# Two edits to a two-layer backbone kernel: the modulation's gates are stored as rows, once per layer, and the output projection multiplies 512 columns per product

## The chip, the cores and the metric

The kernel runs on one core of one Trainium2 chip. The metric is the device time of one execution in microseconds (us). The kernel before takes 1515.74 us, the median of three runs (1512.39, 1515.74 and 1519.95). The profile is that of one further execution, which took 1514.81 us.

The core has a matrix engine (PE in the profile, with its weight loads as PEld), a vector engine (DVE), a scalar engine (ACT), a general engine (POOL), and a synchronising engine (SP) that here only issues transfers. Each runs its own list of instructions in order and waits on semaphores for the others.

## What is computed

Two layers of a backbone over 512 latent tokens and 256 context tokens, 1024 channels wide. Cut to what the change touches:

```python
def trunk_layer(x, xc, mod, mod_c, ...):
    shift, scale, gate = jnp.split(mod[:, None, :], 3, axis=-1)
    shift_c, scale_c, gate_c = jnp.split(mod_c[None, None, :], 3, axis=-1)
    z = split_columns((rmsnorm(x, pre_g) * (1 + scale) + shift) @ w_in)
    ...
    out = merge_branches(z, y_mla, y_pool, y_gla, w_branch_mla, w_branch_pool, w_branch_gla, w_out)
    x = x + gate * rmsnorm(out, post_g)
    if with_ctx_out:
        ...
        xc = xc + gate_c * rmsnorm(out_c, post_g)
    return x, xc

def merge_branches(zz, y_mla, y_pool, y_gla, w_bm, w_bp, w_bg, w_out):
    ...
    merged = g_mla * (y_mla @ w_bm) + g_pool * (y_pool @ w_bp) + g_gla * (y_gla @ w_bg)
    return merged @ w_out

def reference(...):
    for l in range(DEPTH):
        mod = silu_c @ mod_w[l] + mod_b[l]
        mod_c = silu_cc @ mod_w[l] + mod_b[l]
        x, xc = trunk_layer(x, xc, mod, mod_c, ..., l < DEPTH - 1)
```

The gates are `gate` and `gate_c`, the last third of the modulation: 1024 numbers for the latent stream and, in layer 0 only, 1024 for the context stream. The output projection is `merged @ w_out`, 1024 by 1024, over 768 tokens in layer 0 and 512 in layer 1.

## The kernel before

**Products.** Every large product is taken in three: both factors are split into a high and a low part, and `mm3` adds high by high, high by low and low by high into the same PSUM tile (L89 is the one line that issues them). A weight block comes by an SP transfer into a `raw` tile (3 buffers), ACT rounds it to the high part (names that begin with `wh`, L68), and DVE subtracts for the low part (`wl`, L71). There are 4 buffers each for `wh` and `wl`. A product with 128 tokens as the stationary side writes a tile of 128 tokens by as many columns as the weight block is wide.

**Order.** The program is written stage by stage, but a scheduler with a model of times lays out each engine's list, so that work of a later stage (the loads above all) is put between that of an earlier one, and a change of one stage can move instructions of others.

**Modulation.** `mod` is computed in twelve chunks of 256 columns per layer, in the order 0, 4, 1, 5, 2, 6, 3, 7, 8, 9, 10, 11. In layer 0 the first eight run on PE at the start of the program; chunks 8 to 11 of layer 0 (the gates) and all of layer 1 run beside PE: POOL and DVE multiply the weights (`raw_mod`) by one number per partition (L231) and sum them in `macc`, and two small products `modt` turn the sum into columns. `columns(j)` adds the bias and, for the gates, multiplies by the post norm; its result goes to the tile `mcols`, channel `b*128 + p` at partition `p`, column `b`. For the chunks 8 to 11 it then stores the two new columns of each stream to `grow`, an array of rows of 1024 in the chip's memory (L180). Four chunks by two streams make 8 such stores in layer 0, four chunks of one stream make 4 in layer 1.

**Gate rows.** At the start of the output projection `gate_rows` reads `grow` back by POOL, each row broadcast over all 128 partitions (`pg<-grow`, L265): twice in layer 0, once in layer 1.

**Output projection.** `mh` and `ml` are the two parts of the merged activations, with the channels `k` (8 blocks of 128) on the partitions. The weights lie in four column blocks of 256. The first half takes the two blocks of columns 0 to 511 one after the other; in each, the tokens go in pairs of tiles, (2,3), (4,5) and in layer 0 also (0,1), and each pair runs `k` 0 to 5 for both tiles before `k` 6 and 7. ACT copies each tile's 256 columns to `part`. The second half (`wo2` tiles, `wo` in the profile) takes tile after tile, 2 times 256 columns in one PSUM tile. Behind each tile of the second half the norm, the gate (`pg`) and the residual (`xres`, L1069) are applied. In layer 0, `emit_hT` then turns each pair of tiles into columns for layer 1: per `k` two transposes on PE (`xT`, L1098), a scale and shift on DVE (`hv`, L1101), and its high part on ACT (`hh`) and low part on POOL (`hl`).

Of the kernel before, what the change touches and what calls it, by code (L numbers as in the profile page):

```python
# [11 lines left out]
F32 = mybir.dt.float32  # L12
# [6 lines left out]
P = 128  # L19
D = 1024  # L20
KD = 8
# [4 lines left out]
DEPTH = 2  # L26
# [22 lines left out]
def hybrid_kernel(ctx, tc, io, out):  # L49
    nc = tc.nc  # L50
    V, S, G, PE = nc.vector, nc.scalar, nc.gpsimd, nc.tensor
# [8 lines left out]
    stage = ctx.enter_context(tc.tile_pool(name="stage", bufs=2))  # L60
    small = ctx.enter_context(tc.tile_pool(name="small", bufs=4))
    dram = ctx.enter_context(tc.tile_pool(name="dram", bufs=1, space=MemoryType.DRAM))
    psz = ctx.enter_context(tc.tile_pool(name="psz", bufs=2, space=MemoryType.PSUM))
# [3 lines left out]
    def act(out, in_, func=AF.Copy, **kw):  # L67
        return S.activation(out=out, in_=in_, func=func, **kw)  # L68
# [22 lines left out]
    def mm3(out, lh, ll, rh, rl, start, stop):  # L91
        mm(out, lh, rh, start, False)
        mm(out, lh, rl, False, False)
        mm(out, ll, rh, False, stop)
# [17 lines left out]
    def load_split(src, nk, width, name, pool=stream):  # L112
# [4 lines left out]
            split(h, l, raw)  # L117
        return h, l

    def load_block(src, width, name):  # L120

        return [load_split(src[:, 4 * i:4 * i + 4, :], 4, width, f"{name}_{i}") for i in range(2)]
# [32 lines left out]
    def modulation(l, pool=None):  # L155


        cols = const.tile([P, 24, 2], F32, tag=f"mcols{l}", name=f"mcols{l}")
        grow = dram.tile([2, D], F32, name=f"grow{l}")
        mods[l] = (cols, grow)  # L160
        modb = small.tile([P, 24], F32, tag="modb", name=f"modb{l}", bufs=1)
        nc.gpsimd.dma_start(out=modb, in_=io["mod_b"][l])
# [5 lines left out]
        def columns(j, pt, streams=2):  # L168

            at = slice(2 * j, 2 * j + 2)  # L170
            dst = cols[:, at, 0:streams]

            def spread(v, c0):
                return v[:, 2 * j - c0:2 * j - c0 + 2].unsqueeze(2).to_broadcast([P, 2, streams])

            tt(dst, pt[:, :, 0:streams], spread(modb, 0), ALU.add)
            if j >= 8:
                tt(dst, dst, spread(post, 16))
                for st in range(streams):
                    nc.gpsimd.dma_start(out=grow[st].rearrange("(b p) -> p b", p=P)[:, 2 * j - 16:2 * j - 14], in_=dst[:, :, st])  # L180
            elif j >= 4:

                stt(dst, dst, 1.0, spread(pre, 8), ALU.add, ALU.mult)
# [58 lines left out]
        for j in (0, 4, 1, 5, 2, 6, 3, 7, 8, 9, 10, 11):  # L242
            if pool is not None and j < 8:
                chunk_on_pe(j)
            else:
                pend.append(chunk_beside_pe(j))
                next(pend[-1])
                if len(pend) > 1:
                    next(pend.pop(0), None)
            if j == 11 or (pool is None and j == 7):  # L250
                yield
                for chunk in pend:
                    next(chunk, None)
                pend = []
            yield

    mods = {}

    def gate_rows(l, pool, streams):

        grow = mods[l][1]
        res = []
        for s in range(streams):
            pgt = pool.tile([P, D], F32, tag=f"pg{s}", name=f"pg{l}_{s}", bufs=1)
            nc.gpsimd.dma_start(out=pgt, in_=grow[s].partition_broadcast(P))  # L265
            res.append(pgt)
        return res

# [81 lines left out]
    def layer(l, hT, close_hT, side, todo_mod):  # L350
# [683 lines left out]
        part = op.tile([P, NT, 512], F32, tag="part", name=f"part{l}", bufs=1)  # L1034
        order = [2, 3, 4, 5] + ([0, 1] if full else [])
        mT = (mh, ml)
        for b in range(2):
            blk = load_block(io["w_out"][l, b], 256, f"wo{l}_{b}")
            for pair in zip(order[0::2], order[1::2]):
                pss_ = [(psz if t % 2 else psw).tile([P, 256], F32, tag="z" if t % 2 else "w", name=f"zB_wo{l}_{b}_{t}")  # L1040
                        for t in pair]

                for ks in (range(6), range(6, KD)):
                    for t, ps in zip(pair, pss_):
                        for k in ks:
                            wh, wl = blk[k // 4]
                            ts = slice(t * P, t * P + P)
                            mm3(ps, mh[:, k, ts], ml[:, k, ts], wh[:, k % 4, :], wl[:, k % 4, :], k == 0, k == KD - 1)
                for t, ps in zip(pair, pss_):
                    act(part[:, t, b * 256:b * 256 + 256], ps)  # L1050
        ssqs = small.tile([P, NT, 2], F32, tag="ssq_out", name=f"ssq_out{l}", bufs=1)

        for t in order:
            junk = op.tile([P, D], F32, tag="xo", name=f"junk{l}_{t}")
            act(junk[:, 0:512], part[:, t, :], AF.Square, scale=D ** -0.5, accum_out=ssqs[:, t, 0:1])
            tt(part[:, t, :], part[:, t, :], pgr[1 if t < 2 else 0][:, 0:512])
        blks = [load_block(io["w_out"][l, b], 256, f"wo{l}_{b}") for b in (2, 3)]
        xhs = {}
        for t in order:
            ps = psw.tile([P, 512], F32, tag="w", name=f"wo2_{l}_{t}")  # L1060
            ts = slice(t * P, t * P + P)
            for b in range(2):
                for k in range(KD):
                    wh, wl = blks[b][k // 4]
                    mm3(ps[:, b * 256:b * 256 + 256], mh[:, k, ts], ml[:, k, ts], wh[:, k % 4, :], wl[:, k % 4, :],
                        k == 0, k == KD - 1)
            xt = op.tile([P, D], F32, tag="xres", name=f"xres{l}_{t}", bufs=4)
            src = io["ctx"][t * P:t * P + P] if t < 2 else (io["x"] if l == 0 else x1_d)[(t - 2) * P:(t - 1) * P]
            nc.gpsimd.dma_start(out=xt, in_=src)  # L1069
            xo = op.tile([P, D], F32, tag="xo", name=f"xo{l}_{t}")  # L1070
            act(xo[:, 512:], ps, AF.Square, scale=D ** -0.5, accum_out=ssqs[:, t, 1:2])
            tt(xo[:, 512:], ps, pgr[1 if t < 2 else 0][:, 512:])
            ms = small.tile([P, 1], F32, tag="ms1", name=f"ms_post{l}_{t}")

            stt(ms, ssqs[:, t, 0:1], 16 * EPS, ssqs[:, t, 1:2], ALU.add, ALU.add)
            r = small.tile([P, 1], F32, tag="r1", name=f"r_post{l}_{t}")
            tt(r, ms, mhalf[:, 0:1], ALU.pow, G)
            stt(xo[:, 0:512], part[:, t, :], r, xt[:, 0:512], ALU.mult, ALU.add)
            stt(xo[:, 512:], xo[:, 512:], r, xt[:, 512:], ALU.mult, ALU.add)
            if not full:  # L1080
                nc.sync.dma_start(out=out[(t - 2) * P:(t - 1) * P], in_=xo)
                continue
            if t >= 2:
                nc.sync.dma_start(out=x1_d[(t - 2) * P:(t - 1) * P], in_=xo)
            xhs[t] = xhat_tile(xo, xt, op, f"x{l + 1}_{t}")
            if t % 2 == 1:
                emit_hT(nhT, mods[l + 1][0], xhs, t - 1, 2, op)
# [98 lines left out]
def _layout(inp):  # L1186
# [3 lines left out]
    def kblocks(w, n):  # L1190

        dp, kk, nn = w.shape
        return w.reshape(dp, kk // P, P, nn // n, n).transpose(0, 3, 2, 1, 4)
# [36 lines left out]
    d["gla_norm"] = cols(a["gla_norm"])  # L1230
    for n, s in (("m", "mla"), ("p", "pool"), ("g", "gla")):
        d[f"w_branch_{n}"] = kblocks(a[f"w_branch_{s}"], 256)
    d["w_out"] = kblocks(a["w_out"], 256)
    return {f"in_{k}": np.ascontiguousarray(v) for k, v in d.items()}


# [19 lines left out]
```

## Time and profile before

| | us |
|---|---|
| median of three runs | 1515.74 |
| the profiled execution | 1514.81 |
| its span, first to last instruction | 1513.0 |
| around the span | 1.8 |
| PE busy (8940 matmuls) | 1444.7 |
| DVE busy | 1066.7 |
| ACT busy | 717.3 |
| POOL busy | 521.8 |
| mean granted TensorE clock | 0.984 of full |

Matmuls overlap one another in the pipeline, so the spacing of their starts, not their own length, is what one costs. "<-" with a name after a comma gives what ended an idle time; in the view of windows each engine's busy time in the stretch is followed by its count of instructions, then by the granted clock, the share of the 16 DMA engines' time that was taken, and the rate in GB/s. A transfer's landing time is counted from its issue.

### The profile page before, as it was taken

The numbers are of one execution on the slowest core, as the hardware profiler recorded it, in microseconds if no ns is written. First come the engines' busy times: TensorE is split into PE (matmuls) and PEld (weight loads), VectorE is DVE, ScalarE is ACT, GpSimd is POOL, SyncE is SP. The second block draws the span as 40 slices with busy tenths as digits, with TensorE's granted clock in tenths as the row PEclk, the third lists the DMA queues.
The fourth block names the chain that finished last, engine by engine and source line by source line (L and its number), as shares of the span: only waits on it lengthen the run. The fifth ranks groups of instructions, "written<-read, shape, count | busy, mean of one in ns | idle before, by whom it ended". The sixth has DMA issues, their size and how long they took to land.

```text
span 1513.0 us, 23911 instructions
## 1 busy us (share of the span) xinstructions
PE 1444.7 (95%) x8940; PEld 1279.7 (85%) x8940; DVE 1066.7 (71%) x1980; ACT 717.3 (47%) x1340; POOL 521.8 (34%) x695
## 2 busy tenths in 40 slices
PE   7999999999997999997999999999999999998988
PEld 4799899998886889886879988988988888886778
DVE  3645999757576788876676373789976676686783
ACT  6554453343334445666443345654253555454532
POOL 3432333444243443542111064414463100053550
PEclk9999999999998999998999999999999999999999
DMA  9333323256544532346565234334356523157731
GB/s 366 108 125 113 107 96 115 90 166 192 183 74 101 144 118 90 130 147 163 173 210 198 82 126 129 124 127 127 100 180 204 164 96 96 51 151 145 232 132 69
DMA packets 64195, 209.75 MB, mean 139 GB/s; under 512 B 12464, under 2 KB 15696, under 8 KB 64080
## 3 DMA queue, kind: packets, MB, share of 16 engines
q1 hardware_dynamic: 38688, 116.74, 25.2%
q0 software_dynamic: 24528, 88.34, 18.3%
q10 hardware_dynamic: 864, 3.15, 0.5%
q8 instruction: 70, 1.15, 0.3%
q14 instruction: 45, 0.37, 0.1%
HBM read 161.65 MB, written 46.54 MB: 138 GB/s over the span
## 4 chain that ended last, share of the span: by engine, by line
PE 63%; issue 11%; DVE 11%; DMA 8%; POOL 3%; ACT 3%; POOLq 0%; DVEq 0%; SPq 0%; ACTq 0%
PE zA_m L89 13%; PE zB_gv L89 5%; PE zA_px L89 4%; PE zA_mg L89 4%; PE zB_wo L89 4%; PE wo L89 3%; DMA raw_m<-in_w_in 3%; PE lv L89 3%; PE zA_pg L89 3%; PE zA_gk L89 2%; PE br_p L89 2%; PE br_m L89 2%; PE br_g L89 2%; PE zB_qkv L89 2%; PE zA_gq L89 2%
## 5 line engine op out<-in xcount | busy, mean ns | idle before, releaser
L89 PE MATMUL zA_m<-hh,wh_m 128*128 128x512 f32 (+1 forms) x576 | 206.6, 359 | 1.0 <-ACT wh_m L68 1.0
L89 PE MATMUL zA_m<-hh,wl_m 128*128 128x512 f32 (+1 forms) x576 | 206.7, 359 | 0.6 <-DVE wl_m L71 0.6
L89 PE MATMUL zA_m<-hl,wh_m 128*128 128x512 f32 (+1 forms) x576 | 206.5, 359 | 0.0
L89 PEld LDWEIGHTS zA_m<-hh,wh_m 128*128 128x128 f32 x576 | 110.1, 191 | 16.0 <-ACT wh_m L68 1.4
L89 PEld LDWEIGHTS zA_m<-hh,wl_m 128*128 128x128 f32 x576 | 109.9, 191 | 15.6 <-DVE wl_m L71 1.1
L89 PEld LDWEIGHTS zA_m<-hl,wh_m 128*128 128x128 f32 x576 | 109.9, 191 | 14.4
L68 ACT ACTIVATE wh_m<-raw_m 128x1024 fp32r<-128x1024 f32 x48 | 50.9, 1060 | 93.0 <-PE zA_m L89 45.5
L68 ACT ACTIVATE pe<-sc,mx 128x768 f32<-128x768 f32 (+1 forms) x80 | 65.2, 814 | 60.2 <-DVE mx L831 59.7
L831 DVE TENSOR_REDUCE mx<-sc 128x1 f32<-128x768 f32 (+1 forms) x80 | 67.7, 846 | 34.7 <-PE sc L89 34.0
L71 DVE TENSOR_TENSOR wl_m<-raw_m,wh_m 128x1024 fp32r<-128x1024 f32 x48 | 59.0, 1228 | 45.6 <-ACT wh_m L68 45.1
L231 POOL TENSOR_SCALAR raw_mod<-raw_mod,csil 128x256 f32<-128x256 f32 x64 | 69.2, 1085 | 62.0 <-DVE macc L74 38.5
L74 DVE SCALAR_TENSOR_TENSOR macc<-raw_mod,csil,macc 128x256 f32<-128x256 f32 x132 | 70.8, 547 | 12.4 <-POOL macc L71 10.5
L68 ACT ACTIVATE pth<-pt 128x256 fp32r<-128x256 f32 (+1 forms) x144 | 61.8, 471 | 34.6 <-PE pt L853 34.0
L71 DVE TENSOR_TENSOR ptl<-pt,pth 128x256 fp32r<-128x256 f32 (+1 forms) x144 | 72.6, 534 | 7.2 <-ACT pth L68 6.2
L89 PEld LDWEIGHTS lv<-pqk 128*128 128x128 f32 x560 | 70.8, 191 | 4.7 <-issue 1.8
L347 POOL DMA_DIRECT2D sm<-st_m x32 | 17.6, 550 | 165.5 <-ACT st_m L68 148.1
L89 PE MATMUL lv<-pqk 128*128 128x128 f32 x560 | 73.4, 275 | 1.3 <-DVE pqk L71 1.2
L89 PE MATMUL sc<-kth,qth 96*128 96x256 f32 (+1 forms) x144 | 50.8, 353 | 19.0 <-ACT pe L68 18.9
L71 POOL TENSOR_TENSOR macc<-macc,raw_mod 128x256 f32<-128x256 f32 x64 | 55.1, 860 | 36.4 <-DVE macc L74 30.6
L89 PE MATMUL br_p<-yp,wh_wbp 128*128 128x512 f32 (+1 forms) x192 | 56.3, 376 | 8.6 <-ACT yp L68 6.8
L853 PE MATMUL pt<-ident,pe 128*128 128x128 f32 x416 | 61.3, 273 | 0.7 <-ACT pe L68 0.7
L89 PE MATMUL zB_gv<-wh_gv,hh 128*128 128x256 f32 x192 | 55.7, 291 | 4.1 <-ACT st_gv L68 2.1
(402 smaller groups left out, 4732.8 us busy)
## 6 DMA issues: line engine op xcount, KB each, us to landing
raw_mod<-in_mod_w SPq DMA_DIRECT2D x48, 512.0 KB, 5.0
raw_m<-in_w_in SPq DMA_DIRECT2D x48, 512.0 KB, 3.8
sm<-st_m POOLq DMA_DIRECT2D x24, 384.0 KB, 2.9
raw_wo<-in_w_out SPq DMA_DIRECT2D x16, 512.0 KB, 4.0
sm<-st_m POOLq DMA_DIRECT2D x24, 256.0 KB, 2.5
raw_gv<-in_w_gv SPq DMA_DIRECT2D x8, 512.0 KB, 4.6
raw_gg<-in_w_in SPq DMA_DIRECT2D x8, 512.0 KB, 4.0
raw_px<-in_w_in SPq DMA_DIRECT2D x8, 512.0 KB, 3.7
```

The source lines that it names most:

```text
L68: return S.activation(out=out, in_=in_, func=func, **kw)
L71: return (eng or V).tensor_tensor(out=out, in0=a, in1=b, op=op)
L74: return V.scalar_tensor_tensor(out=out, in0=a, scalar=s, in1=b, op0=op0, op1=op1)
L89: PE.matmul(out=out, lhsT=lhsT, rhs=rhs, start=start, stop=stop)
L231: G.tensor_scalar(out=w, in0=w, scalar1=c, scalar2=None, op0=ALU.mult)
L347: nc.gpsimd.dma_start(out=dst[:, lo:T], in_=st[:, lo:T])
L831: V.tensor_reduce(out=mx, in_=ps[:, 0:nkey], axis=AX.X, op=ALU.max, negate=True)
L853: PE.transpose(out=pt[:, kk, :], in_=pe[:, (k0 + kk) * P:(k0 + kk + 1) * P], identity=ident)
```

## The change

First, `columns` no longer stores anything. Once per layer, when chunk 11 has been finished, PE transposes the gate columns in `mcols` (16 of them in layer 0, 8 in layer 1) into a PSUM tile `gateT` of 16 (8) rows of 128 numbers (L262), ACT copies it to the tile `gates`, and one POOL transfer stores those rows to `grow` (L265), whose layout becomes block, stream, channel within the block. The reading back is now one transfer per stream with rows of 128 numbers, 512 bytes, where it was one row of 4 KB; in layer 1, with one stream, the eight pieces lie one behind the other as before.

Second, the output projection's weights are laid out by the host as two halves of 512 columns, each in four quarters of the rows (two `k` each), so that a transfer still brings 512 KB and there are still 8 in each layer. A pair of token tiles goes through the quarters together: both tiles take the two `k` of a quarter before the next quarter, with products 512 columns wide. `part` is written by one ACT copy per tile instead of two. The second half uses the kernel's existing `z_B` with the same blocks.

```diff
+    def load_wide(src, name):
+
+        return [load_split(src[i], 2, 512, f"{name}_{i}") for i in range(4)]
...
-        grow = dram.tile([2, D], F32, name=f"grow{l}")
+        grow = dram.tile([KD, 2 if l < DEPTH - 1 else 1, P], F32, name=f"grow{l}")
...
             if j >= 8:
                 tt(dst, dst, spread(post, 16))
-                for st in range(streams):
-                    nc.gpsimd.dma_start(out=grow[st].rearrange("(b p) -> p b", p=P)[:, 2 * j - 16:2 * j - 14], in_=dst[:, :, st])
...
+            if j == 11:
+
+                n = KD * grow.shape[1]
+                pt = psz.tile([n, P], F32, tag="z", name=f"gateT{l}")
+                columns_ = cols[:, 16:24, :].rearrange("p b s -> p (b s)") if n > KD else cols[:, 16:24, 0]
+                PE.transpose(out=pt, in_=columns_, identity=ident)
+                row = stage.tile([P, P], F32, tag="st", name=f"gates{l}")
+                act(row[0:n], pt)
+                nc.gpsimd.dma_start(out=grow.rearrange("b s p -> (b s) p"), in_=row[0:n])
...
-            nc.gpsimd.dma_start(out=pgt, in_=grow[s].partition_broadcast(P))
+            nc.gpsimd.dma_start(out=pgt.rearrange("q (b p) -> q b p", p=P), in_=grow[:, s].partition_broadcast(P))
...
-        for b in range(2):
-            blk = load_block(io["w_out"][l, b], 256, f"wo{l}_{b}")
-            for pair in zip(order[0::2], order[1::2]):
-                pss_ = [(psz if t % 2 else psw).tile([P, 256], F32, tag="z" if t % 2 else "w", name=f"zB_wo{l}_{b}_{t}")
-                        for t in pair]
-
-                for ks in (range(6), range(6, KD)):
-                    for t, ps in zip(pair, pss_):
-                        for k in ks:
-                            wh, wl = blk[k // 4]
-                            ts = slice(t * P, t * P + P)
-                            mm3(ps, mh[:, k, ts], ml[:, k, ts], wh[:, k % 4, :], wl[:, k % 4, :], k == 0, k == KD - 1)
-                for t, ps in zip(pair, pss_):
-                    act(part[:, t, b * 256:b * 256 + 256], ps)
+        blk = load_wide(io["w_out"][l, 0], f"wo{l}_0")
+        for pair in zip(order[0::2], order[1::2]):
+            pair = [(t, (psz if t % 2 else psw).tile([P, 512], F32, tag="z" if t % 2 else "w", name=f"zB_wo{l}_0_{t}"))
+                    for t in pair]
+
+            for i, (wh, wl) in enumerate(blk):
+                for t, ps in pair:
+                    for k in (2 * i, 2 * i + 1):
+                        ts = slice(t * P, t * P + P)
+                        mm3(ps, mh[:, k, ts], ml[:, k, ts], wh[:, k % 2, :], wl[:, k % 2, :], k == 0, k == KD - 1)
+            for t, ps in pair:
+                act(part[:, t, :], ps)
...
-        blks = [load_block(io["w_out"][l, b], 256, f"wo{l}_{b}") for b in (2, 3)]
+        blk = load_wide(io["w_out"][l, 1], f"wo{l}_1")
...
-            for b in range(2):
-                for k in range(KD):
-                    wh, wl = blks[b][k // 4]
-                    mm3(ps[:, b * 256:b * 256 + 256], mh[:, k, ts], ml[:, k, ts], wh[:, k % 4, :], wl[:, k % 4, :],
-                        k == 0, k == KD - 1)
+            ps = z_B(blk, 0, 512, mT, t, f"wo{l}_1", psw, "w")
```

The scheduler lays the engines' lists out anew. Three places show how.

POOL, in layer 0's attention, where the gate chunks are computed beside PE (`sm` stores a merge gate, `raw_mod` and `macc` are the modulation's weights and sums). Before, at chunk 9, with the stores of chunk 8:

```order
L347 DMA sm_550<-st_m_0_6328 128x768
L231 TENSOR_SCALAR raw_mod_9_0_6333<-raw_mod_9_0_6333,csil 128x256
L180 DMA grow_126<-mcols_125 128x2x1 x2
L71 TENSOR_TENSOR macc_9_6332<-macc_9_6332,raw_mod_9_0_6333 128x256
L231 TENSOR_SCALAR raw_mod_9_0_6333<-raw_mod_9_0_6333,csil 128x256
```

And now, behind chunk 11, where layer 1's chunk 0 has begun (its L233 is L231 of before):

```order
L343 DMA sm_551<-st_m_0_6664 128x768
L890 DMA sgm_0_4466<-sgm_546 128x768
L166 DMA modb_6742<-in_mod_b 128x24
L170 DMA post_6746<-in_post_norm 128x8
L233 TENSOR_SCALAR raw_mod_0_0_6749<-raw_mod_0_0_6749,csil 128x256
L265 DMA grow_126<-gates_6677 16x128
```

Eight stores of 128 by 2 single numbers, spread over four chunks, are now one store of 16 rows behind the last of them.

DVE, in layer 1, where the output projection begins (`mgt_late` and `acc` merge the branches, `ml` is the low part of a merged block `k`). Before, ahead of the first two `ml`:

```order
L71 TENSOR_TENSOR acc_4_14595<-acc_4_14595,mgt_late_15029 128x512
L71 TENSOR_TENSOR wl_wo_1_1_15378<-raw_wo_1_1_15375,wh_wo_1_1_15377 128x1024
L71 TENSOR_TENSOR ml_15164<-acc_1_14592,mh_15163 128x512
L71 TENSOR_TENSOR acc_6_14597<-acc_6_14597,mgt_late_15031 128x512
L71 TENSOR_TENSOR acc_7_14598<-acc_7_14598,mgt_late_15031 128x512
L71 TENSOR_TENSOR ml_15164<-acc_3_14594,mh_15163 128x512
```

And now:

```order
L74 SCALAR_TENSOR_TENSOR mgt_late_14729<-mgt_late_14729,br_m_256_14923 128x512
L71 TENSOR_TENSOR ml_14862<-acc_1_14288,mh_14861 128x512
L71 TENSOR_TENSOR acc_4_14291<-acc_4_14291,mgt_late_14727 128x512
L74 SCALAR_TENSOR_TENSOR mgt_late_14729<-mgt_late_14729,br_m_256_14931 128x512
L71 TENSOR_TENSOR wl_wo_0_3_14972<-raw_wo_0_3_14969,wh_wo_0_3_14971 128x1024
L71 TENSOR_TENSOR ml_14862<-acc_3_14290,mh_14861 128x512
```

The first `ml` stood behind three `acc` sums of the even blocks and the low part of a weight block; now it stands ahead of that weight block and of the sum of block 4.

PE, in layer 0, at the end of the output projection, where the products of the last token tile end (`xT` are the transposes for layer 1, `zA_gq` is layer 1's first product). Before:

```order
L89 MATMUL wo_0_1_9534<-wh_wo_3_1_9079,ml_8014 128x256
L1098 MATMUL xT_2_9425<-ident,xres_4_9324 128x128
L1098 MATMUL xT_2_9425<-ident,xres_5_9392 128x128
L1098 MATMUL xT_3_9432<-ident,xres_4_9324 128x128
L1098 MATMUL xT_3_9432<-ident,xres_5_9392 128x128
```

And now:

```order
L89 MATMUL zB_wo_1_1_9254<-wh_wo_1_3_8919,ml_8010 128x512
L1101 MATMUL xT_4_9039<-ident,xres_2_8948 128x128
L1101 MATMUL xT_4_9039<-ident,xres_3_8992 128x128
L1101 MATMUL xT_5_9046<-ident,xres_2_8948 128x128
L1101 MATMUL xT_5_9046<-ident,xres_3_8992 128x128
L1101 MATMUL xT_6_9053<-ident,xres_2_8948 128x128
L1101 MATMUL xT_6_9053<-ident,xres_3_8992 128x128
```

Before, the last product has the transposes of tiles 4 and 5 from `k` = 2 behind it; those of tiles 2 and 3 and two of tiles 4 and 5 stand among the products. Now four groups of the tiles 2 and 3 (`k` 4 to 7) and all of the tiles 4 and 5 stand behind the last product, seven groups (the first three of the tiles 4 and 5 among them) ahead of layer 1's first one.

More of the change, by code (lines that the diff above doesn't have):

```diff
@@ L1056, in layer @@
             tt(part[:, t, :], part[:, t, :], pgr[1 if t < 2 else 0][:, 0:512])
-        blks = [load_block(io["w_out"][l, b], 256, f"wo{l}_{b}") for b in (2, 3)]
+        blk = load_wide(io["w_out"][l, 1], f"wo{l}_1")
         xhs = {}
         for t in order:
-            ps = psw.tile([P, 512], F32, tag="w", name=f"wo2_{l}_{t}")
-            ts = slice(t * P, t * P + P)
-            for b in range(2):
-                for k in range(KD):
-                    wh, wl = blks[b][k // 4]
-                    mm3(ps[:, b * 256:b * 256 + 256], mh[:, k, ts], ml[:, k, ts], wh[:, k % 4, :], wl[:, k % 4, :],
-                        k == 0, k == KD - 1)
+            ps = z_B(blk, 0, 512, mT, t, f"wo{l}_1", psw, "w")
             xt = op.tile([P, D], F32, tag="xres", name=f"xres{l}_{t}", bufs=4)
@@ L1232, in _layout @@
         d[f"w_branch_{n}"] = kblocks(a[f"w_branch_{s}"], 256)
-    d["w_out"] = kblocks(a["w_out"], 256)
+    d["w_out"] = a["w_out"].reshape(DEPTH, 4, 2, P, 2, 512).transpose(0, 4, 1, 3, 2, 5)
     return {f"in_{k}": np.ascontiguousarray(v) for k, v in d.items()}
```

## Prediction

> **What bounds the kernel now.** First the page's head, its busy times and its chain of work that ended last:
>
> ```profile
> span 1513.0 us, 23911 instructions
> PE 1444.7 (95%) x8940; PEld 1279.7 (85%) x8940; DVE 1066.7 (71%) x1980; ACT 717.3 (47%) x1340; POOL 521.8 (34%) x695
> PE 63%; issue 11%; DVE 11%; DMA 8%; POOL 3%; ACT 3%; POOLq 0%; DVEq 0%; SPq 0%; ACTq 0%
> ```
>
> PE is the bound, at 95%: only 1513.0 − 1444.7 = 68 us are left in which it does nothing, and DMA has 8% of the chain, a large share for an engine whose work should be ahead. So a change can win in two ways: fewer microseconds of products, or fewer of those 68. I therefore went to the waits of PE and asked of each long one what ended it and what stood before. The longest is at 452 us, in layer 0's attention. Here the waits of the stretch 440 to 465 (us in total, times, longest), POOL's row ahead of it in the timeline, and the transfer's landing time, in that stretch and as the median of the whole run:
>
> ```profile
> PE sc L89 <- ACT pe L68: 10.2, 1, 10.2
> ACT wh_m L68 <- DMA raw_m<-in_w_in: 14.7, 2, 13.9
> 443.70 1.48 POOL L180 DMA_DIRECT2D grow<-mcols  x2
> raw_m<-in_w_in SPq DMA_DIRECT2D x1, 512.0 KB, 16.2
> raw_m<-in_w_in SPq DMA_DIRECT2D x48, 512.0 KB, 3.8
> ```
>
> PE waits 10.2 us for the softmax's exponential on ACT; ACT stands 13.9 us at the head of its list for a weight block; and that block landed after 16.2 us where its like take 3.8. It was issued less than a microsecond behind two gate stores. The view of windows (the stretch and its length, the busy time and count of PE, PEld, DVE, ACT and POOL, the granted clock, the DMA engines' share and their GB/s) shows what the DMA engines did meanwhile, and the cost after:
>
> ```profile
> 445.00:453.00 8.00, 7.65 (x45) 6.56 (x43) 6.92 (x12) 1.08 (x3) 2.72 (x4) 1.00 1.11 39
> 453.00:460.00 7.00, 0.00 (x0) 0.00 (x0) 0.00 (x0) 0.00 (x0) 0.00 (x0) 0.73 0.70 113
> 462.00:468.00 6.00, 5.13 (x23) 4.85 (x24) 5.52 (x11) 2.87 (x7) 2.85 (x4) 0.63 0.25 87
> ```
>
> From 445 to 453 all 16 DMA engines are taken the whole time and move 39 GB/s; at 706 to 712, in a row below, a share of 0.76 moves 256. From 453 on, no compute engine runs anything. Behind it the granted clock is 0.63 for six microseconds. The same picture stands behind the stores at 692.75 and 1363.63:
>
> ```profile
> 692.75 0.74 POOL L180 DMA_DIRECT2D grow<-mcols  x1 [0.32 <-DVE mcols L71]
> PE br_p L89 <- ACT yp L68: 6.8, 1, 6.8
> 695.17 10.41 DMA yrp<-yp
> 696.00:704.00 8.00, 2.36 (x15) 1.97 (x15) 1.23 (x5) 1.93 (x3) 0.06 (x1) 0.87 0.76 43
> 706.00:712.00 6.00, 5.71 (x16) 4.50 (x17) 4.89 (x11) 5.43 (x13) 0.58 (x1) 0.50 0.76 256
> ```
>
> ```profile
> 1363.63 0.75 POOL L180 DMA_DIRECT2D grow<-mcols  x1
> ACT wh_wbp L68 <- DMA raw_wbp<-in_w_branch_p: 13.5, 2, 10.0
> PE sc L89 <- ACT pe L68: 4.8, 1, 4.8
> PE br_p L89 <- ACT wh_wbp L68: 1.3, 1, 1.3
> 1366.00:1374.00 8.00, 7.32 (x39) 5.92 (x37) 3.77 (x7) 0.05 (x1) 1.31 (x3) 1.00 1.01 35
> 1378.00:1384.00 6.00, 5.52 (x16) 4.66 (x17) 5.78 (x10) 4.49 (x10) 3.05 (x4) 0.50 0.57 166
> ```
>
> Three of the longest waits of PE, then, 10.2, 6.8 and 4.8 us, each begin some 6 to 10 us behind a gate store, with the DMA engines taken and moving 35 to 43 GB/s, and each is followed by some 6 us at 0.50 to 0.63 of the clock. A store writes 128 times 2 single numbers of 4 bytes, 256 pieces. I take it that the pieces hold the DMA engines for about 8 us per store.
>
> **The change part by part.** The sum is made against the profiled execution, 1514.8 us (span 1513.0 and 1.8 around it); the median of the runs is 0.9 us higher, which is inside their own spread of 7.6.
>
> *The twelve stores go.* POOL's own time for them is not worth anything:
>
> ```profile
> L180 POOL DMA_DIRECT2D grow<-mcols x12: 716/742/776, 426.4 to 1387.1; - x12
> 483.39 1.51 POOL L180 DMA_DIRECT2D grow<-mcols  x2
> 491.00:499.00 8.00, 8.00 (x65) 7.70 (x64) 6.78 (x16) 2.63 (x7) 2.58 (x4) 1.00 0.86 143
> ```
>
> 12 × 0.742 = 8.9 us leave POOL, which is busy 34% of the span; behind it stands modulation work that nothing waits for soon. Nor does every store cost PE something: as far behind the pair at 483.39, PE is busy 8.00 of 8 us. What counts are the three waits. At 452: had the block landed after 3.8 us, at 448.3, ACT would have had it some 4 us before PE ran dry; 10.2 us, and (1 − 0.63) × 6 = 2.2 of clock, 12.4 together; DVE is busy 6.92 of 8 us there and comes next, so I take **11**. At 699: the transfer took 10.41 us; at about the 3.8 of the weight block it ends near 699, and PE waits for little; 6.8 and (1 − 0.50) × 6 = 3.0 make 9.8, taken **8.5**. At 1373: 4.8 and 1.3, and 3.0 of clock, make 9.1, taken **7.5**, since the branch weights there land after some 4.5 us in the whole run's median:
>
> ```profile
> raw_wbp<-in_w_branch_p SPq DMA_DIRECT2D x8, 512.0 KB, 4.5
> ```
>
> Together −27. If the cover is thinner than I think (each wait's other half is due to a later item in the same list), half of it stays: −13.
>
> *The projection's products.* Starts of 512-wide and of 256-wide products, 20 steps apart each:
>
> ```profile
> 446.28 0.40 PE L89 MATMUL zA_m<-hh,wl_m 128*128 128x512 f32 x1
> 450.84 0.39 PE L89 MATMUL zA_m<-hl,wh_m 128*128 128x512 f32 x1
> ```
>
> ```profile
> 822.03 0.28 PE L89 MATMUL zB_wo<-wh_wo,mh 128*128 128x256 f32 x1
> 824.39 0.28 PE L89 MATMUL zB_wo<-wh_wo,ml 128*128 128x256 f32 x1
> ```
>
> 4.56 / 20 = 0.228 us against 2.36 / 20 = 0.118. 960 products of 256 become 480 of 512 (layer 0: 576 to 288, layer 1: 384 to 192), each saving 2 × 0.118 − 0.228 = 0.008: 480 × 0.008 = 3.8, taken **−3.5**. If a pair of short ones costs no more than a long one, it is 0. The Trainium skill, "TensorE: Matmul & The Clock Gate", section "Wait — 56ns, not 53.3ns?", gives a start-to-start time of N / 2.4 GHz plus about 2.5 ns for a warm array, so that halving the count would save an estimated 480 × 2.5 ns = 1.2 us only, and the forecast by it would be 2.3 us higher; this trace's rows show wider steps for both widths, and the sum goes by them.
>
> *Layer 1's start of the projection.* DVE and PE at 1456 to 1464:
>
> ```profile
> 1456.00:1464.00 8.00, 4.64 (x31) 3.83 (x31) 8.00 (x8) 3.65 (x6) 7.33 (x5) 1.00 0.66 259
> PE zB_wo L89 <- DVE ml L71: 2.4, 1, 2.4
> 1459.88 2.32 DVE L71 TENSOR_TENSOR wl_wo<-raw_wo,wh_wo 128x1024 fp32r<-128x1024 f32 x1
> ```
>
> PE is idle 8 − 4.64 = 3.4 us there, 2.4 of it for the first `ml`, which stood behind a weight block's low part of 2.32 us. In the new list of DVE the first `ml` stands ahead of the low part next to it, which is the fourth quarter's, and PE has three quarters, 3 × 2 tiles × 2 `k` × 3 = 36 products, before it needs that one: **−2.5**. What is late next is the second `ml` behind that low part, so between 0 and −3.4.
>
> *Layer 0's end.* Behind the last product stood six groups of transposes, four of them ahead of layer 1's first product; now there are twelve and seven. POOL's `hl` and PE's wait for DVE's `hv` set their pace:
>
> ```profile
> L71 POOL TENSOR_TENSOR hl<-hv,hh 128x256 fp32r<-128x256 f32 x8 | 8.6, 1096 | 0.4 <-ACT hh L68 0.4
> 896.14 1.14 PE L1098 MATMUL xT<-ident,xres 128*128 128x128 f32 x4 [3.48 <-DVE hv L1101]
> ```
>
> Before, PE waited 3.48 us there. Six more groups at 1.1 us each now come there; layer 1's first products take the groups as they come and hide most of it. Between 0 and six more groups, 6 × 1.1 = 6.6; **+2**.
>
> *One store per layer, a transpose and a copy come.* The store has 16 (8) pieces of 512 bytes, for which no row of this trace stands; between nothing and the price of an old store it is nearest to nothing by its count of pieces, 16 of 256, so 0; the upper end is a wait like that at 1373 in each layer, 9.6. The transpose stands in PE's list behind the last `modt`, whose columns DVE still has to finish; the page has no such wait, so between 0 and PE's wait for `hv` above in each layer, 7.0; DVE's step there is one small addition of a few numbers per partition, far less than the 2.32 of a whole `wl`, so **+1** for the two layers.
>
> *Sum:* −27 + 1 − 3.5 − 2.5 + 2 = −30, to 1485. A list that is laid out anew from 420 us on will put some other wait where one has gone; no row of before can show it. I hold back 3 us (one wait of the size of that at 896) and forecast **1488 us**.
>
> **The rivals.** *The stores are not the cause.* The Trainium skill, "DMA: Bandwidth & Descriptors", section "Anatomy of one DMA — SWDGE (gpsimd) path", gives a fixed cost of about 2.0 us and bytes over 436 GB/s, by which a store of 1 KB is over after an estimated 2.0 us and holds nobody; its waits would belong to the loads. The traces say otherwise:
>
> ```profile
> grow<-mcols POOLq DMA_DIRECT2D x12, 1.0 KB, 9.4
> up<-zqk POOLq DMA_DIRECT2D x22, 128.0 KB, 2.8
> ```
>
> A store of 1 KB lands after 9.4 us in the median, and one of 128 KB in 256 pieces of 512 bytes after 2.8. If all the same the slow loads were slow by themselves, the terms left are +1 − 3.5 − 2.5 + 2 = −3: 1512. The changed kernel would show its loads at 440, 695 and 1366 landing late without a store. *Half of it only:* the waits shrink, but the next item in each list is late too: −13 in place of −27, 1485 + 14 + 3 = 1502 with the 3 held back. *The slower side: the read-back is now the slow transfer.* It is broadcast to 128 partitions in eight pieces each, 1024 pieces of 512 bytes, where 4 KB rows were read:
>
> ```profile
> pg<-grow POOLq DMA_DIRECT2D x3, 512.0 KB, 4.7
> 816.87 0.53 POOL L265 DMA_DIRECT2D pg<-grow  x1 [1.46 <-PE br_g L89]
> 858.35 0.69 DVE L71 TENSOR_TENSOR part<-part,pg 128x512 f32<-128x512 f32 x1
> ```
>
> If a piece costs what a piece of the old stores does, 9.4 / 256 = 0.037 us, each read-back takes 37.6 us instead of 4.7; the two of layer 0 run one behind the other from 816.9 and end at 892, and the last tile's gate, needed at 858.4, comes 34 us late; the second half's weight loads share the same engines. 1488 + 34 = 1522. It decides from 2 × x − 41.5 = 27, x = 34 us per read-back, on. Against it speaks the transfer of 256 pieces of 512 bytes in 2.8 us. *The change doesn't do what it says* cannot well be: the new lists hold no store of single numbers.
>
> **How the numbers follow.** Forecast (1478 to 1495) 0.72; half of it (1495 to 1507) 0.16; not the cause (1507 to 1516) 0.08; read-back or an equal loss 0.04 above. The lower end is all terms at their far end, −12.4 − 9.8 − 9.1 − 3.8 − 3.4 = −38.5, to 1476, which I don't expect to come together: 1478. The upper end takes in the half: 1505. A difference of over 0.5% (7.6 us) is about what a measurement of this kernel can tell from no change: faster has 0.87 of the chance (the forecast and nearly all of the half), within 0.5% 0.09, slower 0.04.
>
> **What would show it.** Right: no stretch behind 440, 695 and 1366 in which the DMA engines are taken and move under 50 GB/s; the weight blocks there land after about 4 us; PE's longest waits are under 5 us; DMA's 8% of the chain falls to about 6; 8460 matmuls and two transposes, with steps of 0.228 in the projection. Wrong: waits of 5 us or more at the same places with other releasers (half), late loads without a store (not the cause), `pg<-grow` landing after over 30 us (slower side), or PE waiting more than 6 us between the last product of layer 0 and layer 1's first.

## The result and the profile after

The changed kernel takes **1496.9 us** (median of six runs, 1494.7 to 1499.2), the kernel before 1515.2 in the same comparison: ratio 0.9875, with a 95% interval of 0.9857 to 0.9894. Forecast were 1488 and a range of 1478 to 1505. It is faster, as forecast, by 18 us where 27 were expected. Timed once more beside other kernels, it stood at 1498.8 (0.9896, 0.9874 to 0.9919).

First the head of the page, the busy times and the chain that ended last, in the profiled execution of 1494.7 us:

```profile
span 1493.0 us, 22952 instructions
PE 1437.4 (96%) x8462; PEld 1253.2 (84%) x8462; DVE 1068.1 (72%) x1980; ACT 717.0 (48%) x1332; POOL 524.7 (35%) x685
PE 59%; DVE 13%; issue 13%; DMA 6%; POOL 5%; ACT 3%; POOLq 0%; DVEq 0%; SPq 0%; ACTq 0%
```

DMA's share of the chain fell from 8% to 6% and DVE's rose from 11% to 13%. PE does nothing for 1493.0 − 1437.4 = 55.6 us, against 68.3 before: 12.7 us less. The waits that I had priced away came to 25.5 (10.2, 6.8, 4.8, 1.3 and 2.4), so about half of them came back somewhere.

The three stalls themselves are gone. Here PE's waits from 425 us to the projection of layer 0, the DMA issues from 436 to 460 and, in a second piece, from 675 to 700, and the window that stands where the first stall was:

```profile
PE sc L89 <- ACT pe L68: 4.0, 5, 1.8
PE br_m L89 <- DVE mgt_m L74: 3.3, 3, 1.8
PE pt L864 <- ACT pe L68: 1.4, 1, 1.4
...
PE br_p L89 <- ACT yp L68: 0.2, 1, 0.2
```

```profile
raw_m<-in_w_in SPq DMA_DIRECT2D x2, 512.0 KB, 3.7
...
raw_wbp<-in_w_branch_p SPq DMA_DIRECT2D x4, 512.0 KB, 3.4
yrp<-yp SPq DMA_DIRECT2D x4, 384.0 KB, 3.6
```

```profile
440.00:460.00 20.00, 20.00 (x127) 17.96 (x126) 18.25 (x38) 10.24 (x22) 11.23 (x10) 1.00 0.35 111
```

No wait of PE is longer than 1.8 us there, where 10.2 and 6.8 stood; the two weight blocks land after 3.7 us in the median, where one took 16.2, and the four `yrp` after 3.6, where the one behind the store took 10.4; and from 440 to 460 PE is busy throughout, with a DMA share of 0.35 that moves 111 GB/s.

What came in is behind the projection of layer 0. The windows of 26 us that begin with the end of its last product, before (first) and after (second):

```profile
891.80:917.80 26.00, 22.50 (x102) 18.21 (x103) 16.25 (x23) 11.55 (x23) 14.91 (x20) 0.93 0.39 129
```

```profile
874.70:900.70 26.00, 19.45 (x81) 14.42 (x79) 14.97 (x23) 8.23 (x19) 15.34 (x21) 0.80 0.34 119
```

And, of after, the waits there, PE's for the scale and shift of the transposed tiles and DVE's for the context's residual tile:

```profile
PE xT L1101 <- DVE hv L1104: 6.5, 5, 2.9
DVE xo L74 <- DMA xres<-in_ctx: 3.1, 1, 3.1
```

PE does 81 matmuls there instead of 102 and is idle 6.55 us instead of 3.50, and the clock is 0.80 instead of 0.93, another 0.13 × 26 = 3.4 us.

A table by stage says where the time went. Each stage is measured between the starts (or ends) of the first (or last) product of its kind in the timeline; the first point is one product at 325 us in the list of before, up to which PE's list is the same in all:

| stage, us | before | after | after, again | forecast of the difference |
|---|---|---|---|---|
| start, to the same product | 325.1 | 327.9 | 326.8 | 0 |
| to layer 0's projection | 496.6 | 479.8 | 485.3 | −19 |
| layer 0's projection | 70.1 | 67.0 | 68.0 | −2.1 |
| from its end to layer 1's pooling input (`zA_px`) | 118.8 | 127.0 | 125.8 | +2 |
| to layer 1's merge gates (`zA_m`) | 125.2 | 127.4 | 129.1 | 0 |
| to layer 1's projection | 320.3 | 311.1 | 310.8 | −7 |
| layer 1's projection | 49.9 | 45.6 | 45.6 | −3.9 |
| to the end | 7.1 | 7.2 | 7.2 | 0 |

### The profile page after: what moved, and what is told of

It is laid out like the page before. It is cut to its first block, busy times and chain, and to the rows that moved or that the text cites. A ratio compares the mean times of both kernels' runs of the same rounds, so it can differ in the third digit from the quotient of the medians.

```text
span 1493.0 us, 22952 instructions
## 1 busy us (share of the span) xinstructions
PE 1437.4 (96%) x8462; PEld 1253.2 (84%) x8462; DVE 1068.1 (72%) x1980; ACT 717.0 (48%) x1332; POOL 524.7 (35%) x685
## 4 chain that ended last, share of the span: by engine, by line
PE 59%; DVE 13%; issue 13%; DMA 6%; POOL 5%; ACT 3%; POOLq 0%; DVEq 0%; SPq 0%; ACTq 0%
PE zA_m L89 12%; PE zB_wo L89 6%; PE zB_gv L89 5%; PE zA_mg L89 4%; PE br_g L89 3%; PE br_m L89 3%; PE zA_pg L89 2%; PE zA_gk L89 2%; PE lv L89 2%; PE zB_qkv L89 2%; PE zA_px L89 2%; PE br_p L89 2%; DVE pqk L71 2%; PE zA_gq L89 2%; PE modps L89 2%
## 5 line engine op out<-in xcount | busy, mean ns | idle before, releaser
L233 POOL TENSOR_SCALAR raw_mod<-raw_mod,csil 128x256 f32<-128x256 f32 x64 | 77.6, 1215 | 49.8 <-DVE macc L74 25.7
L89 PE MATMUL zB_wo<-wh_wo,ml 128*128 128x512 f32 x160 | 61.8, 393 | 1.2 <-POOL ml L71 1.2
L89 PE MATMUL zB_wo<-wl_wo,mh 128*128 128x512 f32 x160 | 62.1, 392 | 0.0
L89 PE MATMUL zB_wo<-wh_wo,mh 128*128 128x512 f32 x160 | 61.8, 391 | 0.0
```

Of the source, the lines that this page charges most:

```text
L89: PE.matmul(out=out, lhsT=lhsT, rhs=rhs, start=start, stop=stop)
L233: G.tensor_scalar(out=w, in0=w, scalar1=c, scalar2=None, op0=ALU.mult)
```

## The experiments

Two parts of one change, so first each by itself, and then the stores put back beside the whole change.

**The first part alone.** One row store per layer, the projection of before.

```diff
-                for st in range(streams):
-                    nc.gpsimd.dma_start(out=grow[st].rearrange("(b p) -> p b", p=P)[:, 2 * j - 16:2 * j - 14], in_=dst[:, :, st])
+            if j == 11:
...
+                PE.transpose(out=pt, in_=columns_, identity=ident)
+                row = stage.tile([P, P], F32, tag="st", name=f"gates{l}")
+                act(row[0:n], pt)
+                nc.gpsimd.dma_start(out=grow.rearrange("b s p -> (b s) p"), in_=row[0:n])
```

> The change's first part alone: one row store per layer, the output projection as before. Theory A (the element stores hold the DMA engines; the loss of 8 us at layer 1's start, seen in the changed kernel's profile, belongs to the wide projection): the three long waits at 452, 699 and 1373 go and nothing is given back, about 1491 (ratio 0.984), faster than the full change. Theory B (the loss at layer 1's start comes with any new layout of the lists): about 1500 (0.990). Rival (the slow loads are slow by themselves): 1515 (1.000), with a wait over 5 us at each of the three places.

Measured: 1493.2 us, ratio 0.9848 (0.9814 to 0.9882). Theory A's side: the gain is here, 22 us, and nothing is given back at layer 1's start (118.2 us in that stage, against 118.8 before and 127.0 in the full change). So Theory B, by which any new layout of the lists brings that loss, is out. The forecast for this part alone, −27 + 1, was 4 too high.

**The second part alone.** Wide products, the twelve element stores as before.

```diff
-            blk = load_block(io["w_out"][l, b], 256, f"wo{l}_{b}")
...
+        blk = load_wide(io["w_out"][l, 0], f"wo{l}_0")
...
+                        mm3(ps, mh[:, k, ts], ml[:, k, ts], wh[:, k % 2, :], wl[:, k % 2, :], k == 0, k == KD - 1)
...
+            ps = z_B(blk, 0, 512, mT, t, f"wo{l}_1", psw, "w")
```

> The change's second part alone: products 512 wide by quarters, the gates stored element by element as before. Theory A: the projection itself gains 3 + 4.5 us, layer 1's start loses 8 to 10, the three long waits stay: about 1516 (1.001). Theory B: about 1508 (0.995). Rival (the stores are not the cause): the full change's gain comes from here, 1497 (0.988).

Measured: 1523.2 us, ratio 1.0057 (1.0035 to 1.0079): by itself the wide projection makes the kernel **slower**, by 8 us, where 1 was expected. Its stage at layer 1's start takes 128.6 us, 9.8 more than before, and the next one 127.5, 2.3 more; the projections take 68.0 (70.1) and 49.1 (49.9). The stores' waits are still there, in ACT's row for the weight block in the stretch 440 to 470 and PE's for `yp` at 690 to 712:

```profile
ACT wh_m L68 <- DMA raw_m<-in_w_in: 10.1, 2, 8.9
...
PE br_p L89 <- ACT yp L68: 6.1, 1, 6.1
```

**The full change with the stores put back, into an array that nobody reads.**

```diff
+        spare = dram.tile([2, D], F32, name=f"spare{l}")
...
+                for st in range(streams):
+                    nc.gpsimd.dma_start(out=spare[st].rearrange("(b p) -> p b", p=P)[:, 2 * j - 16:2 * j - 14], in_=dst[:, :, st])
```

> The full change, and beside it the twelve element stores as before, into an array that nobody reads. Theory A: each store lands after about 9 us, the DMA engines behind it move under 50 GB/s, and where a load follows PE waits again; all waits back gives 1497 + 22 = 1519, and as the lists stand differently anything from 1505 up; the loads next to the stores must land after 8 us or more. Rival: 1497, loads in 4 us.

Measured: 1526.7 us, ratio 1.0068 (1.0038 to 1.0098): 28 to 30 us more than the full change, although nothing waits for these stores' data. That is 7.7 above the forecast; the nearer comparison is the second part alone, which has the same stores and takes 3.4 us less, with intervals that overlap. Here two of the stores in the timeline, the window behind them, the landing times from 440 to 462, and PE's waits up to the projection:

```profile
445.13 1.48 POOL L185 DMA_DIRECT2D spare<-mcols  x2
```

```profile
447.00:455.00 8.00, 8.00 (x48) 7.08 (x48) 7.83 (x13) 1.75 (x5) 3.06 (x3) 1.00 0.99 27
```

```profile
raw_m<-in_w_in SPq DMA_DIRECT2D x1, 512.0 KB, 11.4
spare<-mcols POOLq DMA_DIRECT2D x2, 1.0 KB, 9.5
```

```profile
PE sc L89 <- ACT pe L68: 10.0, 3, 5.5
PE br_p L89 <- ACT yp L68: 6.4, 1, 6.4
```

The engines are taken (0.99) and move 27 GB/s, the load that follows lands after 11.4 us, and PE's waits are back at the first two places. That settles the cause of the stalls: it is the stores, not the loads and not the layout of the lists.

**What in the stores costs it: two forms of layer 0's stores, in the kernel before.** In the first, both streams of a chunk go in one transfer of 128 pieces of 16 bytes.

```diff
-        grow = dram.tile([2, D], F32, name=f"grow{l}")
+        grow = dram.tile([P, KD, 2] if l == 0 else [2, D], F32, name=f"grow{l}")
...
+                if l == 0:
+                    nc.gpsimd.dma_start(out=grow[:, 2 * j - 16:2 * j - 14, :], in_=cols[:, at, :])
```

> The kernel before, with layer 0's eight stores of 256 pieces of 4 bytes made four of 128 pieces of 16 bytes (both streams of a chunk in one; the gates then come back in another order, which is left so); layer 1 as before, as its own control. If the cost goes by pieces: a store lands after about 5 us instead of 9, the pair's 13 us become 5, the waits at 452 and 699 nearly go, the one at 1373 stays: 1515 - 18 = 1497 (0.988). If it goes by the store, whatever its pieces: half of the waits stay, 1508 or more, and a store still lands after 9 us.

Measured: 1503.7 us, ratio 0.9925 (0.9903 to 0.9948). A store landed after 1.8 us (the last of the four after 2.5), less than either theory had, so neither held as it stood. In the second form the pieces are the same 256 of 4 bytes as before, only at other addresses.

```diff
-                    nc.gpsimd.dma_start(out=grow[:, 2 * j - 16:2 * j - 14, :], in_=cols[:, at, :])
+                    for st in range(streams):
+                        nc.gpsimd.dma_start(out=grow[:, 2 * j - 16:2 * j - 14, st], in_=dst[:, :, st])
```

> As the kernel with 16-byte pieces, but each of layer 0's eight stores again in 256 pieces of 4 bytes, written 64 bytes apart from partition to partition where the kernel before writes neighbouring partitions 4 bytes apart (the gates come back in another order; layer 1 as before). If the size or the number of the pieces sets the cost: a store lands after about 9 us and the wait at 452 is back, 1514 (1.000). If it was the neighbouring addresses: about 2 us, and 1504 as with 16-byte pieces (0.993).

Measured: 1505.4 us, ratio 0.9931 (0.9905 to 0.9958). The stores, the window behind them and the landing times from 440 to 462:

```profile
446.58 1.48 POOL L181 DMA_DIRECT2D grow<-mcols  x2
```

```profile
448.00:456.00 8.00, 8.00 (x49) 7.12 (x48) 7.94 (x15) 3.87 (x7) 3.40 (x5) 1.00 0.39 106
```

```profile
raw_m<-in_w_in SPq DMA_DIRECT2D x2, 512.0 KB, 3.2
grow<-mcols POOLq DMA_DIRECT2D x2, 1.0 KB, 3.2
```

As many pieces, as small, PE's products in the very order of the kernel before, and yet this pair lands after 3.2 us (the other three pairs of layer 0 after 2.0, 2.2 and 4.7 in the median), the DMA share is 0.39, and the loads take 3.2 us. So it is neither the number nor the size of the pieces: it is that, in `grow` of before, 128 partitions write 4 bytes each to **neighbouring addresses**. From the product at 325 us to layer 0's projection the two forms take 482.3 and 480.0 us, against 496.6 before and 479.8 in the full change: other addresses are enough for the gain there. Both forms give the gates back in another order, so they serve for the times alone. In both forms layer 1's four stores were left as they were, and its waits stayed: in the second form PE waits 6.3 us at 686 (layer 1's first store falls into layer 0's attention) and up to 3.4 near 1360, by its rows of waits in 680 to 700 and 1340 to 1370:

```profile
PE br_p L89 <- ACT yp L68: 6.3, 1, 6.3
...
PE sc L89 <- ACT pe L68: 4.3, 2, 3.4
```

**Why the wide projection costs at layer 1's start.** The order of PE's list suggests it: of the 48 transposes that feed layer 1, 20 stand ahead of the projection's last product before, 8 in the full change. The full change's trace shows one way by which late transposes come back to PE. POOL issues the load of the context's residual tile only when transposes have freed a buffer for it; DVE waits for that tile, and the `hv` behind it in DVE's list comes late to PE:

```profile
877.80 1.16 POOL L1072 DMA_DIRECT2D xres<-in_ctx  x2 [1.01 <-PE xT L1101]
883.60 0.75 DVE L74 SCALAR_TENSOR_TENSOR xo<-part,r_post,xres 128x512 f32<-128x512 f32 x1 [3.13 <-DMA xres<-in_ctx]
885.52 0.69 PE L1101 MATMUL xT<-ident,xres 128*128 128x128 f32 x2 [2.91 <-DVE hv L1104]
```

The same wait of DVE, 3.2 to 4.4 us, stands in the three other profiles with 8 transposes ahead and these four buffers (the full change again, the second part alone, the stores put back), and in none with 18 or 20.

Two kernels put the transposes back, by making only the second half narrow: on the same wide loads, or with its own loads of before. The width of the products and the transposes' places change together in both.

```diff
-            ps = z_B(blk, 0, 512, mT, t, f"wo{l}_1", psw, "w")
+            ps = psw.tile([P, 512], F32, tag="w", name=f"wo2_{l}_{t}")
+            ts = slice(t * P, t * P + P)
+            for c in (0, 256):
+                for k in range(KD):
+                    wh, wl = blk[k // 2]
+                    mm3(ps[:, c:c + 256], mh[:, k, ts], ml[:, k, ts], wh[:, k % 2, c:c + 256], wl[:, k % 2, c:c + 256],
+                        k == 0, k == KD - 1)
```

> The full change, but the second half's products are 256 columns wide again, two per weight tile, on the same wide loads and with the same quarters. Theory C (the loss at layer 1's start comes from the transposes' places in PE's list: with wide products in the second half 8 of 48 transposes stand ahead of the last product, here 18 as before about 20): layer 1's start wins back 8 to 10 us and the products lose 240 x 0.008 = 1.9: about 1489 (0.983). Rival D (it comes from the wide loads, four quarters that the first tile must wait for, or from the first half): no change, 1497 (0.988).

> The full change, but the second half as before in whole: blocks of 256 columns with their own loads (20 of 48 transposes ahead of the last product). Theory C: as with the narrow second half, about 1489 (0.983). Rival D, if the loads are at fault: this one gains, 1489, and the one with narrow products on wide loads doesn't, 1497. If the first half is at fault: neither, 1497.

Measured: 1491.9 (0.9845, 0.9807 to 0.9883) and 1503.4 us (0.9922, 0.9894 to 0.9949). In the stage itself both gave most of the loss back, 121.8 and 119.8 us against 127.0, with 118.8 before. Since the transposes move over the border between the projection and this stage, the two together tell more: 188.9 us before, 194.0 and 193.8 in the full change, 196.6 with the second part alone, 189.9 and 188.3 here. Here the first one's window of 26 us behind its last product, and PE's waits in it:

```profile
872.00:898.00 26.00, 22.25 (x110) 18.15 (x110) 17.85 (x27) 10.81 (x21) 15.80 (x21) 0.87 0.34 122
```

```profile
PE xT L1107 <- DVE hv L1110: 3.7, 3, 1.4
```

PE is busy 22.25 us of 26, as before the change (22.50), and the wait for `hv` is 3.7 us instead of 6.5. The total of the second kernel missed its forecast by 14 us, though, and what it lost lies in other places: the next stage took 131.2 us (125.2 before), and the one to layer 1's projection 318.6 (311.1 in the full change), at the end of which PE waited for DVE and the clock was low:

```profile
PE zB_wo L89 <- DVE gated L74: 4.8, 1, 4.8
```

```profile
1438.00:1446.00 8.00, 3.19 (x11) 2.34 (x10) 8.00 (x10) 2.10 (x3) 3.56 (x3) 0.75 0.37 124
```

Is it the residual tile's wait alone, or the transposes' places without it? Six buffers take DVE's 3.1 us away:

```diff
-            xt = op.tile([P, D], F32, tag="xres", name=f"xres{l}_{t}", bufs=4)
+            xt = op.tile([P, D], F32, tag="xres", name=f"xres{l}_{t}", bufs=6)
...
-            v = pool.tile([P, n], F32, tag="hv", name=f"hv_{k}_{t0}", bufs=4)
+            v = pool.tile([P, n], F32, tag="hv", name=f"hv_{k}_{t0}", bufs=3)
```

> The full change with six buffers for the residual tiles in place of four (and three for hv in place of four, to make room), so that the context tiles' loads wait for no transposes. Theory E (the loss is DVE's wait for these loads, 3.1 us in the changed kernel's profile, with what hangs behind it): about 1490 (0.983). Theory C: DVE's wait goes but the transposes stand as late as before, 8 of 48 ahead of the last product; 1495 (0.987).

Measured: 1507.4 us, ratio 0.9953 (0.9937 to 0.997), slower than the full change. DVE's wait for the residual tile is gone, but the stage takes 126.1 us as before, and PE's wait for `hv` is longer:

```profile
PE xT L1101 <- DVE hv L1104: 8.2, 4, 3.4
```

So taking the tile's wait away did not give the loss back, with 8 transposes ahead as in the full change. That speaks for the places themselves, but doesn't settle it: the three buffers for `hv` and the lists, laid out anew, may have made the longer wait, which wasn't tried apart. The rest of what this kernel lost lies in other stages, the most to layer 0's projection (3.5 us more than the full change), to layer 1's merge gates (3.7) and to layer 1's projection (2.5).

**All together on one chip, and a version that keeps what gained.** Since only layer 0's projection is followed by transposes, the last kernel makes only layer 1's wide.

```diff
+        if full:
+            for b in range(2):
+                blk = load_block(io["w_out_n"][b], 256, f"wo{l}_{b}")
...
+        else:
+            blk = load_wide(io["w_out_w"][0], f"wo{l}_0")
```

> The full change, timed again on the same chip as the next three: 1497 (0.988).

> The first part alone, again. If the projection part costs what it showed alone against the kernel before (8.4 us) this one is faster than the full change by about that less what the lists' new layout moves: 1492 against 1497. If it costs nothing beside the first part: equal within 3 us.

> The full change with the second half 256 columns wide, again: 1492 (0.985), 4 to 5 us below the full change if the transposes' places are the cause, equal to it within 3 us if the first look was chance.

> The first part, and the wide projection in layer 1 only, where no transposes follow; layer 0's projection as before (20 of 48 transposes ahead of the last product). If wide products cost only at layer 1's start: faster than the first part alone by the 3 us that layer 1's projection gained (48.6 to 45.6), about 1490 (0.983), and layer 1's start as short as before (119 us from the projection's end to the pooling input's first product). If the order of the other stages shifts as much as in the other kernels: 1490 to 1500.

| kernel | us | ratio to before | 95% interval |
|---|---|---|---|
| the full change | 1498.8 | 0.9896 | 0.9874 to 0.9919 |
| the first part alone | 1493.3 | 0.9858 | 0.9832 to 0.9883 |
| the second half narrow | 1493.8 | 0.9873 | 0.9851 to 0.9894 |
| wide in layer 1 only | **1489.2** | 0.9837 | 0.9813 to 0.9860 |

The last is clear of the full change, by 9.6 us, and its intervals overlap those of the two between. Its stages are as expected: 118.7 us at layer 1's start (118.8 before, 127.0 in the full change) and 45.6 for layer 1's projection (49.9 before). The median of the first part alone lies below that of the full change in both comparisons, by 3.8 and 5.5 us, though each pair of intervals overlaps a little.

## Why the prediction was right, and by how much not

The time lies within the range and moved as forecast, but it lies 9 us above the forecast, in the part (1495 to 1507, at 0.16) that the prediction had given to the rival by which half of the waits stay. That the sum came no worse is in part luck: layer 0 gained less than was priced and lost more at its end and behind it, layer 1 gained 2 us more, and 3 us had been held back for waits that no row of before showed.

**The stalls (−27).** The mechanism is shown: the stores hold the DMA engines, and three waits of PE go with them. The size was too large in layer 0. To the projection the full change gained 16.8 and 11.3 us in two profiled executions, and the first part alone 10.7; 19 were forecast (11 and 8.5, less half of the transposes' 1). Two things were missed. The next waits: at 460 to 480 PE, which had worked throughout before, is idle 20 − 18.23 us, and at 680 to 692, just ahead of the second place, it is idle 2.5:

```profile
460.00:480.00 20.00, 18.23 (x116) 16.25 (x115) 13.33 (x30) 9.08 (x19) 5.78 (x7) 1.00 0.36 116
680.00:692.00 12.00, 9.50 (x46) 8.09 (x44) 9.92 (x24) 8.10 (x22) 4.96 (x7) 0.72 0.67 201
```

And the clock: I priced 8.2 us of half clock behind the stalls as gone. The mean granted clock went from 0.984 to 0.986, which is (1 − 0.984) × 1513 = 24.2 us lost before and (1 − 0.986) × 1493 = 20.9 after: 3.3 us, a measure that counts idle time at the low clock too. Other stretches of low clock came: one with the new waits, the 0.72 in the second row, and more at layer 1's start (below). The first part alone shows the like, 0.987 and 0.986 in its two profiles. In layer 1 the term was right or a little small: −9.2 in the stage, 7 forecast.

**The added transpose, copy and store (+1).** Nearly right. PE waited 1.8 us at layer 1's transpose and not at layer 0's, and the new store lands after 2.9 us in layer 0 (shown) and 4.9 in layer 1:

```profile
495.52 0.38 PE L262 MATMUL gateT<-ident,mcols 128*16 128x128 f32 x1
...
1371.58 0.28 PE L262 MATMUL gateT<-ident,mcols 128*8 128x128 f32 x1 [1.81 <-DVE mcols L71]
```

```profile
grow<-gates POOLq DMA_DIRECT2D x1, 8.0 KB, 2.9
```

**The products (−3.5) and layer 1's start of the projection (−2.5).** Their sum, −6.0, stands against −7.4 and −6.4 measured in the two projections. How much of it the width brought isn't shown. In layer 0 the projection of before took 70.1 and 68.1 us in two executions of the first part alone, and the wide one 67.0 and 68.0, with 12 transposes fewer in it. In layer 1 the full change took 45.6 both times, the first part alone 48.6 and 50.0; but with the second part alone it was 49.1, with PE still waiting 2.7 us for DVE's first `ml`. So long a wait for an `ml` is gone only in the lists that have the first part; in the full change 1.2 us for an `ml` by POOL stand there. 512-wide products start 0.229 us apart, 18 steps from the first to the second row:

```profile
811.80 0.39 PE L89 MATMUL zB_wo<-wh_wo,mh 128*128 128x512 f32 x1
815.92 0.39 PE L89 MATMUL zB_wo<-wh_wo,ml 128*128 128x512 f32 x1
```

**Layer 0's end (+2).** This is the step that failed, in its size and in its reach: "layer 1's first products take the groups as they come and hide most of it". They hid less than that. Ahead of layer 1's first product PE is idle about as long as before (1.60, 0.61, 1.15 and 0.27 us, where 3.48 stood in one piece). What came in is the wait of 2.91 us behind layer 1's first three products, shown above, for an `hv` that stood behind the residual tile's late load, and low clock. The stage lost 8.2 us (7.0 in the second profile, 9.8 with the second part alone): in the window of 26 us 3.05 more idle and 3.4 of lower clock, and transposes that had stood among the products. A second stretch of low clock follows in the same stage, where the window of before that covers the like (937 to 957) had 15.32 us of PE at 0.83:

```profile
925.00:945.00 20.00, 13.95 (x85) 13.09 (x85) 9.94 (x33) 13.75 (x20) 4.88 (x10) 0.75 0.46 139
```

The stage behind it lost 2.1 to 6.0 us more in all eight profiles with wide products in layer 0's projection, which I had not looked for. Its cause is open: with the second half narrow it stayed long (129.1, 127.3 and 131.2 us, against 125.2 before). Against the kernel before, the second part by itself is therefore a loss of 8 us and not the gain of 4 that I had; beside the first part it costs 4 to 5.5 by the medians. I had read the order of the list and priced six groups of transposes at 1.1 us; what I did not price is the buffer that late transposes keep from the residual tile, the low clock, and the stage behind.

**The rivals.** "The stores are not the cause" is out, by the stores put back. With it goes, for this kernel, the reading by the fixed cost and the rate in the Trainium skill, "DMA: Bandwidth & Descriptors", section "Anatomy of one DMA — SWDGE (gpsimd) path": its estimate of 2.0 us for 1 KB comes near the 4-byte stores at 64-byte steps, 2.0 to 4.7 us for the four pairs above, and is far from those at neighbouring addresses, at 9.5. The slow read-back is out: `pg<-grow` lands after 5.4 us in layer 0 with its 512-byte pieces, 4.8 before, far from the 34 us at which it would have decided. "Half of it only" lay nearest, not because half of each stall stayed but because other waits took their place.

## What to carry to other kernels

Look for tiny stores whose neighbouring words come from different partitions: they cost 0.74 us of POOL each where they are issued and can stall the loads that follow, so their price stands in another engine's waits. Time the parts of a change apart: here one part won 22 us and the other lost 8 by itself, and together they looked like one moderate gain. Fewer and wider products need not be a gain if other work had been laid among the old ones; count in the list of the new kernel what now stands behind the last product, ask which buffer it keeps busy, and price the clock with it.

## What had not been expected of the hardware

The stall depends on addresses: 256 pieces of 4 bytes at neighbouring addresses landed after about 9.5 us with the DMA engines at a share of 0.99 and 27 GB/s, and as many at 64-byte steps from partition to partition after 2.0 to 4.7 us, with the engines at 0.39 and 106 GB/s behind the pair shown. Why neighbouring words are slow wasn't shown. The stage from 325 us to layer 0's projection differed by 5.5 us between two profiled executions of the same changed kernel (479.8 and 485.3), more than most of the terms that are argued about here. Why the scheduler lays the transposes later with wide products in the second half isn't known either.
